# Three of layer 1's modulation groups, computed on VectorE beside layer 0's feed-forward network

## The chip, the core and the metric

The kernel runs on one core of a Trainium2 chip. A core has five engines, each with an instruction queue of its own that it works through in order: TensorE (PE, matrix products; its weight loads are shown apart as PEld), VectorE (DVE), ScalarE (ACT), GpSimd (POOL) and SyncE (SP), which in this kernel issues all DMA transfers. [...] The metric is the device time of one execution in microseconds (us), as the median over several runs.

## The reference

The model is a two-layer backbone over 512 latent tokens with 256 context tokens in front, width 1024. Layer 0 mixes with latent attention (8 heads) and an RWKV-7 recurrence; layer 1 with a state-space scan and windowed attention. Each layer then has a gated feed-forward network. Every norm is modulated by vectors that come from a conditioning vector, one for the latent tokens (c) and one for the context (c_ctx):

```python
def adaln_mods(cond, p):
    return jnp.split(jax.nn.silu(cond) @ p['ada_w'] + p['ada_b'], 6, axis=-1)

def trunk_layer(x_lat, x_ctx, c, c_ctx, p, mixer, rope, need_ctx):
    m_lat = [m[:, None, :] for m in adaln_mods(c, p)]
    m_ctx = adaln_mods(c_ctx, p)
    o_ctx, o_lat = mixer(modulate(x_ctx, p['norm_mix_g'], m_ctx[0], m_ctx[1]),
                         modulate(x_lat, p['norm_mix_g'], m_lat[0], m_lat[1]), p, rope, need_ctx)
    x_lat = x_lat + m_lat[2] * o_lat
    x_lat = x_lat + m_lat[5] * conv_ffn(modulate(x_lat, p['norm_ffn_g'], m_lat[3], m_lat[4]), p)
    if need_ctx:
...
```

So each layer has six groups of 1024 modulation values for each of two conditioning vectors: a product of a 2 x 1024 matrix with a 1024 x 6144 matrix of float32 weights, 4 MB per group. Group 0 is the shift and group 1 the scale of the mixer's norm, group 2 the gate on the mixer's output, groups 3 to 5 the same for the network. In the last layer the context's output isn't needed, so of its groups only 0 and 1 are used.

## The kernel before

Activations lie with features on the 128 partitions and tokens along the free axis (256 context tokens, then 512 latent ones, 768 in all). A float32 product is made of three faster ones: each operand is split into a rounded high part (a copy on ACT) and a remainder (a subtraction on DVE); helper split, lines 386 to 388, does it for activations and load_w, lines 320 to 327, for weights (raw tile wraw, parts whi and wlo; two raw buffers, three split ones).

The modulation of a group is made by ada_group (line 391). For each of 8 blocks of input features it loads a 128 x 1024 weight tile aw (512 KB, line 399) and issues four matmuls into 32-row strips of one PSUM bank; then DVE copies the sums (am, line 404), PE transposes them in two matmuls (line 407) and DVE adds the bias into mods (line 409). The matmuls go through helper mm, so their line is 267.

The program's order is not the written one: a scheduler reorders instructions within each engine by its own estimates, under data dependencies and under explicit ties (issue_after). What the final queue of an engine holds is therefore read from the built program.

The stages that matter here:

- Layer 0's recurrence and attention, about 500 to 735 us of the profiled execution. The recurrence (tiles rec, u, t, b) steps through chunks of 64 tokens in two directions, each step fed by loads of 1 MB (rec) and 128 KB (u). The eight attention heads (tiles kh, qh, ax, ab, pt, o) are interleaved with it on PE. After each of the heads 0, 1 and 2 stands a call of ada_group for layer 1's groups 0, 1 and 2, with a PSUM bank named ad and two aw buffers in a pool aw1.
- The output projection of layer 0, about 735 to 809 us.
- Layer 0's feed-forward network, function ffn, about 810 to 1378 us. Its prenorm has a fill: the call of ada_group for layer 1's group 3 (pool aw2, five buffers). Then it goes through 22 pairs of up tiles in groups of 6, 6, 5 and 5. For each tile PE makes 48 matmuls into one of three accumulators acc; conv3 (lines 380 to 383) drains it with one pass on ACT and two on DVE for each of the two token segments. After each pair come a Silu on ACT, a product on DVE (line 1151) and a split (line 388 on DVE). After each group come eight down tiles, whose results DVE adds to the residual (line 484). The weights are prepared up to three tiles ahead.
- Layer 1's prenorm, from about 1378 us, which needs groups 0 and 1 of mods1, with the call for group 4 (late) beside it.

The few lines that call ada_group:

```python
        if h < 3:
            ada_group(1, h, mods1, "aw1", 2)
...
    ffn(0, mods0, xs, SEG2, NTOK, "left", lambda: ada_group(1, 3, mods1, "aw2", 5))
...
    ada_group(1, 4, mods1, "aw2", 5, late=True)
```

Of the kernel before, what the change touches and what calls it, by code (L numbers as in the profile page):

```python
# [10 lines left out]
F32 = mybir.dt.float32  # L11
F32R = mybir.dt.float32r
AF = mybir.ActivationFunctionType
# [115 lines left out]
def layout(inp):  # L129
# [4 lines left out]
    cc = np.stack([g["c"][0], g["c_ctx"]], 1)  # L134
    a["cc"] = cc.reshape(KT, P, 2).transpose(1, 0, 2)
    a["ada"] = g["ada_w"].reshape(2, KT, P, 6, 1024).transpose(0, 3, 1, 2, 4)
    ab = g["ab_w_in"][0]
    krs = np.concatenate([ab[:, 656:672], ab[:, 640:656]], 1)
    rw = ab[:, 672:]
# [71 lines left out]
def hybrid_kernel(ctx: ExitStack, tc: tile.TileContext, a, out):  # L211
# [44 lines left out]
    ptt = nc.gpsimd.tensor_tensor  # L256

    pace = dict(pins=None, per=0.0, t=0.0, base=0)
    pe_last = [None]

    def mm(o, lhsT, rhs, start, stop, shared=False):
        i = -1
# [122 lines left out]

    def split(hi, lo, src):
        nc.scalar.copy(hi, src)  # L387
        tt(out=lo, in0=src, in1=hi.bitcast(F32), op=ALU.subtract)


    def ada_group(layer, grp, mods, pool, bufs, bank_=None, late=False):
        b = (bank_ or bank)()
        s_ = sc
        if late:
            s_ = F()[:, :KT * 32].rearrange("p (k c) -> p k c", c=32)
            nc.gpsimd.tensor_copy(s_, sc)
        for k in range(KT):
            w = T(pool, [P, 1024], "aw", bufs)
            dma(w, a["ada"][layer, grp, k])
            for g in range(4):  # L400
                mm(b[32 * g:32 * g + 32, :256], lhsT=s_[:, k], rhs=w[:, 256 * g:256 * g + 256], start=k == 0,
                   stop=k == KT - 1)
        am = T(pool, [P, 256], "am", 1)
        nc.vector.tensor_copy(am, b[:, :256])
        b = b[:, 256:]
        for q in range(2):
            nc.tensor.transpose(b[:, q * P:(q + 1) * P], am[:, q * P:(q + 1) * P], ident)
        o = PV[f"ada_b{layer}"] + 8 * grp
        tt(out=mods[:, 8 * grp:8 * grp + 8].rearrange("p (g q) c -> p q g c", q=2),
           in0=b[:, :256].rearrange("p (q g r) -> p q g r", q=2, r=32)[:, :, :, 0:2],  # L410
           in1=pv[:, o:o + 8].rearrange("p (g q) -> p q g", q=2).unsqueeze(3).to_broadcast([P, 2, 4, 2]), op=ALU.add)

    def rstd(ps, n_el, epsi, t0=0, n=NTOK, po=PO, r=None):
        r = F() if r is None else r
# [577 lines left out]
    identr = T("at", [P, P], "identr", 1, F32R)  # L992
    nc.scalar.copy(identr, ident)

    open_pool("aw1", "right")

    def att_load(h):

        t = {}
# [71 lines left out]
    for h in range(8):  # L1071
        cur = nxt
        if h + 1 < 8:
            nxt = att_load(h + 1)
        if h % 2 == 0:
            ot = F()
        att_head(h, ot, *cur)
        if h % 2 and h < 7:
            spill(f"att{h // 2}", ot)
        if h < 3:  # L1080
            ada_group(1, h, mods1, "aw1", 2)
    close_pool("aw1", "at", "mla", "ad", "ob", "ab", "ax")
    open_acc("accm", 2)

    paced(None, 0, 0)
# [28 lines left out]
    close_pool("rwb", "rw1", "rw0", "misc")  # L1114


    def ffn(layer, mods, xs, segs, width, side, fill, nsegs=None, r=None):
        open_pool("ffn", side)

        def S(dt=F32):  # L1120
# [10 lines left out]
        for gsz in FG[layer]:  # L1131
            us, ul = [], []
            halves = layer and j0 + gsz == FT
            for j in range(j0, j0 + gsz):
                cv = []
                for jj in (j, FT + j):
                    ps = acc()
                    dense(ps, next_w("up"), P, hh, hl, segs=segs, by_pass=j < 2)
                    o = S()
                    conv3(o, ps, ALL, col(f"conv_w{layer}0", jj), col(f"conv_w{layer}1", jj), col(f"conv_w{layer}2", jj),  # L1140
                          col(f"conv_b{layer}", jj), segs)
                    cv.append(o)
                    if halves:
                        raw = T("sb", [P, 8, P], "wraw", NWR)
                        dma(raw[:, :gsz], a["down"][layer, len(wb)][:, j0:])
                        hi, lo = [T("hold", [P, 4, P], "w", 16, F32R) for _ in range(2)]
                        split(hi, lo, raw[:, :gsz])
                        wb.append((hi, lo))
                gt, vl = cv
                act(gt[:, n0:], gt[:, n0:], AF.Silu)  # L1150
                tt(out=vl[:, n0:], in0=gt[:, n0:], in1=vl[:, n0:], op=ALU.mult)  # L1151
                hi, lo = S(F32R), S(F32R)
                split(hi[:, n0:], lo[:, n0:], vl[:, n0:])
                us.append(hi)
                ul.append(lo)
            if halves:
                break
            for m in range(8):
                ps = acc()
                dense(ps, next_w("down"), P, us, ul, nk=gsz, segs=segs)  # L1160
                resid(xs[m], ps, mods, 5, m, segs)
            j0 += gsz
# [29 lines left out]
        close_pool("ffn")  # L1192

    open_pool("aw2", "right")
    ffn(0, mods0, xs, SEG2, NTOK, "left", lambda: ada_group(1, 3, mods1, "aw2", 5))


    open_pool("h1", "left")
# [1 line left out]
    for k in range(KT):  # L1200
        dma(xsp[:, k], xs[k][:, L0:L1])
    hh, hl = prenorm(xs, mods1, "norm_mix_g1", 0, 1, lambda: row_tile("h1", "h", 16, F32R), lambda k: xs[k], add=ptt, npool=3)
    ada_group(1, 4, mods1, "aw2", 5, late=True)
    close_pool("aw2", "xs0", "b0", "acc")
    open_pool("sd", "right", psum=True)
    accp[:] = ["acc1", 2, 1024]
# [424 lines left out]
```

## Time and profile before

| | us |
|---|---|
| median of 3 runs | 2265.78 (2265.28 to 2267.42) |
| the profiled execution | 2264.21 |
| its span, first to last instruction | 2262.3 |
| PE busy | 2076.5 |
| DVE busy | 1346.3 |
| ACT busy | 928.3 |
| POOL busy | 506.2 |

The profile is one execution, written down by the hardware. Busy times are of the span; an engine that is busy nearly all the time in a stage sets the pace there, and idle time of another engine costs nothing. Views used below: the page (busy time by engine, the chain of work that ended last), windows (busy time of each engine in stretches of the span, with the granted clock of PE, the busy share of the DMA engines and GB/s), groups of equal instructions with their mean duration, the timeline (start, duration, engine, line, operation, and in brackets the idle time before it and what ended it) and the list of waits (us in total, times, longest).

### The profile page before, as it was taken

How to read it: one execution, taken by the hardware profiler on the slowest of the kernel's cores; microseconds unless marked ns; L12 is line 12 of the kernel's file. 1: busy time of each engine (PE TensorE's matmuls, PEld its weight loads, DVE VectorE, ACT ScalarE, POOL GpSimd, SP SyncE). 2: the span in 40 equal slices, each digit the busy share in tenths (PEclk: the TensorE clock that was granted, in tenths of full speed). 3: DMA queues.
4: the chain of work that ended last, by engine and by line, in shares of the span. 5: the costliest groups of instructions: out<-in, count | busy, mean ns of one | idle time of the engine just before them, and what ended most of it. 6: DMA issues, size and time to landing. Idle time of an engine off the chain costs nothing.

```text
span 2262.3 us, 33884 instructions
## 1 busy us (share of the span) xinstructions
PE 2076.5 (92%) x13558; PEld 1640.9 (73%) x13558; DVE 1346.3 (60%) x2081; ACT 928.3 (41%) x1434; POOL 506.2 (22%) x486
## 2 busy tenths in 40 slices
PE   5888889788998999999999998898888999999997
PEld 3666667566654878888888886786565667888886
DVE  5566965666766465445354444678985556554555
ACT  4445663532355244233132335544344345342434
POOL 0027686611223010000000004442641230000000
PEclk9999999698999999999999999999889999999998
DMA  8477777669741441211212213213426032323231
GB/s 303 125 206 206 182 211 195 211 190 320 259 165 42 154 139 62 61 66 57 75 53 60 75 58 114 96 52 117 133 71 172 28 111 79 96 92 98 84 116 61
DMA packets 181069, 282.58 MB, mean 125 GB/s; under 512 B 63328, under 2 KB 118656, under 8 KB 177840
## 3 DMA queue, kind: packets, MB, share of 16 engines
q1 hardware_dynamic: 180912, 280.42, 40.6%
q8 instruction: 107, 1.75, 0.3%
q14 instruction: 50, 0.41, 0.1%
HBM read 225.43 MB, written 47.33 MB: 121 GB/s over the span
## 4 chain that ended last, share of the span: by engine, by line
PE 65%; DVE 6%; ACT 5%; DMA 5%; issue 3%; POOL 1%; SPq 0%; DVEq 0%; ACTq 0%; POOLq 0%
PE acc L267 49%; PE sd L267 3%; PE o L267 3%; PE wo L267 2%; PE ab L267 2%; PE b L267 2%; DMA u<-sp_v 1%; DVE E L1359 1%; DMA aw<-ada 1%; POOL I L750 1%; PE ax L267 1%; PE ad L267 1%; POOL w L748 1%; DMA E<-sp_ac 1%; ACT L416 1%
## 5 line engine op out<-in xcount | busy, mean ns | idle before, releaser
L267 PE MATMUL acc<-s,whi 128*128 128x512 f32 (+1 forms) x3104 | 759.8, 356 | 3.0 <-ACT s L463 3.0
L267 PEld LDWEIGHTS acc<-s,whi 128*128 128x128 f32 x3104 | 546.0, 188 | 97.3 <-ACT s L463 4.8
L267 PE MATMUL acc<-s,wlo 128*128 128x512 f32 (+1 forms) x1552 | 462.0, 358 | 0.0
L267 PE MATMUL acc<-h,whi 128*128 128x256 f32 (+2 forms) x1248 | 321.1, 371 | 15.9 <-ACT p L639 5.0
L325 ACT CAST whi<-wraw 128x1024 fp32r<-128x1024 f32 (+5 forms) x228 | 210.0, 923 | 282.3 <-PE acc L267 218.0
L267 PEld LDWEIGHTS acc<-s,wlo 128*128 128x128 f32 x1552 | 289.5, 188 | 42.9 <-DVE wlo L326 0.7
L267 PEld LDWEIGHTS acc<-h,whi 128*128 128x128 f32 (+1 forms) x1248 | 223.7, 197 | 68.4 <-issue 15.4
L326 DVE TENSOR_TENSOR wlo<-wraw,whi 128x1024 fp32r<-128x1024 f32 (+5 forms) x205 | 218.7, 1069 | 44.2 <-ACT whi L325 43.6
L381 DVE SCALAR_TENSOR_TENSOR s<-acc,pv,s 128x511 f32<-128x511 f32 (+1 forms) x132 | 87.0, 659 | 246.2 <-ACT s L380 245.4
L380 ACT ACTIVATE s<-acc,pv 128x512 f32<-128x512 f32 (+1 forms) x132 | 93.4, 708 | 235.4 <-PE acc L267 224.2
L484 DVE SCALAR_TENSOR_TENSOR x<-acc,mods,x 128x512 f32<-128x512 f32 (+1 forms) x136 | 79.4, 620 | 175.0 <-PE acc L267 174.8
L267 PE MATMUL acc<-h,wlo 128*128 128x256 f32 (+2 forms) x624 | 179.5, 362 | 0.0
L434 POOL TENSOR_TENSOR f<-f,f 128x768 f32<-128x768 f32 (+1 forms) x24 | 31.3, 1306 | 635.0 <-ACT f L429 625.1
L267 PEld LDWEIGHTS acc<-h,wlo 128*128 128x128 f32 (+1 forms) x624 | 119.3, 195 | 21.9 <-issue 5.6
L1178 POOL TENSOR_TENSOR s<-w,s 128x256 f32<-128x256 f32 x6 | 5.0, 855 | 381.3 <-ACT s L416 381.3
L383 DVE SCALAR_TENSOR_TENSOR s<-acc,pv,s 128x511 f32<-128x511 f32 (+1 forms) x132 | 87.2, 660 | 4.2
L750 POOL TENSOR_TENSOR I<-I,w 128x30 f32<-128x30 f32 (+14 forms) x120 | 76.7, 639 | 9.0
L748 POOL TENSOR_TENSOR w<-I 128x30 f32<-128x30 f32 (+14 forms) x120 | 69.4, 578 | 34.6 <-PE iv L267 25.8
L387 ACT CAST s<-s 128x768 fp32r<-128x768 f32 (+1 forms) x44 | 32.0, 727 | 106.1 <-DVE s L1151 106.1
L326 POOL TENSOR_TENSOR wlo<-wraw,whi 128x1024 fp32r<-128x1024 f32 x23 | 61.7, 2686 | 59.6 <-ACT whi L325 56.1
L1359 DVE TENSOR_SCALAR E<-E,acm 128x128 f32<-128x128 f32 x128 | 61.2, 546 | 14.6 <-ACT G L1356 14.6
L723 DVE TENSOR_TENSOR W<-gk,con 64x512 f32<-64x512 f32 x48 | 32.8, 683 | 51.2 <-ACT PB L722 47.3
(390 smaller groups left out, 3347.3 us busy)
## 6 DMA issues: line engine op xcount, KB each, us to landing
aw<-ada SPq DMA_DIRECT2D x96, 512.0 KB, 5.8
wraw<-up SPq DMA_DIRECT2D x88, 512.0 KB, 3.5
rec<-sp_rec SPq DMA_DIRECT2D x24, 1024.0 KB, 9.7
wraw<-w_in SPq DMA_DIRECT2D x47, 512.0 KB, 3.8
wraw<-down SPq DMA_DIRECT2D x40, 384.0 KB, 3.1
sp_rec<-tg SPq DMA_DIRECT2D x24, 384.0 KB, 3.3
E<-sp_ac SPq DMA_DIRECT2D x16, 512.0 KB, 5.5
x<-xT SPq DMA_DIRECT2D x16, 384.0 KB, 5.9
```

Of the source, the lines that this page charges most:

```text
L267: ins = nc.tensor.matmul(o, lhsT=lhsT, rhs=rhs, start=start, stop=stop, skip_group_check=shared)
L325: nc.scalar.copy(hi[:, :kt], raw[:, :kt])
L326: (eng or tt)(out=lo[:, :kt], in0=raw[:, :kt], in1=hi[:, :kt].bitcast(F32), op=ALU.subtract)
L380: act(o[rows, t0:t0 + n], ps[rows, po:po + n], AF.Identity, scale=w1, bias=b)
L381: stt(out=o[rows, t0 + 1:t0 + n], in0=ps[rows, po:po + n - 1], scalar=w0, in1=o[rows, t0 + 1:t0 + n], op0=ALU.mult, op1=ALU.add)
L383: stt(out=o[rows, t0:t0 + n - 1], in0=ps[rows, po + 1:po + n], scalar=w2, in1=o[rows, t0:t0 + n - 1], op0=ALU.mult, op1=ALU.add)
L387: nc.scalar.copy(hi, src)
L484: stt(out=x[:, t0:t0 + n], in0=ps[:, po:po + n], scalar=mods[:, c6 * 8 + m, c:c + 1], in1=x[:, t0:t0 + n], op0=ALU.mult, op1=ALU.add)
L723: tt(out=w[hk], in0=b[hk].rearrange("p c (a t) -> p c a t", a=2), in1=mk[hk].rearrange("p (a t) -> p a t", a=2).unsqueeze(1).to_broadcast( ...
L748: eng.tensor_tensor(out=tmp, in0=I[:, m + 1:, m:m + 1].to_broadcast([P, n, m]), in1=I[:, m:m + 1, :m].to_broadcast([P, n, m]), op=ALU.mult)
L750: eng.tensor_tensor(out=I[:, m + 1:, :m], in0=I[:, m + 1:, :m], in1=tmp, op=ALU.add)
L1359: ts(out=e[:, h], in0=e[:, h], scalar1=acm[:, c, h0 + h:h0 + h + 1], scalar2=0.0, op0=ALU.subtract, op1=ALU.min)
```

## The change

Groups 0, 1 and 2 of layer 1 are no longer made by ada_group. The weights of these groups are also laid out transposed by the host-side layout (ada1t: 24 tiles of 128 outputs x 1024 inputs), and a new generator ada_rows makes one tile per step: a load of the tile (512 KB) and one scalar_tensor_tensor on DVE that multiplies it with the conditioning vector (srow, loaded to all partitions and put through Silu on ACT) and sums each row into one column of mods1. There are 16 such rows for the context and 24 for the latent tokens, 40 in all, and one addition of the bias after each of the two parts. In ffn of layer 0, from the second pair of up tiles on, two steps of the generator follow each split, and each row is tied behind the split's subtraction on DVE. The pool aw1 goes, and aw2 has four buffers in place of five, plus one for srow.

```diff
@@ layout
+    a["ada1t"] = g["ada_w"][1][:, :3 * D].T.reshape(24, P, D)
+    a["ccrow"] = np.stack([g["c"][0], g["c_ctx"]], 0)
@@ split
-        tt(out=lo, in0=src, in1=hi.bitcast(F32), op=ALU.subtract)
+        dve_last[0] = tt(out=lo, in0=src, in1=hi.bitcast(F32), op=ALU.subtract).ins
@@ new
+    def ada_rows(mods, pool, bufs):
+
+        for c in (1, 0):
+            sr = T(pool, [P, D], "srow", 1)
+            dma(sr, a["ccrow"][c:c + 1].partition_broadcast(P))
+            act(sr, sr, AF.Silu)
+            nt = 16 if c else 24
+            for n in range(nt):
+                w = T(pool, [P, D], "aw", bufs)
+                dma(w, a["ada1t"][n])
+                with tc.issue_after(dve_last[0]):
+                    stt(out=w, in0=w, scalar=1.0, in1=sr, op0=ALU.mult, op1=ALU.mult, accum_out=mods[:, n, c:c + 1])
+                yield
+            tt(out=mods[:, :nt, c], in0=mods[:, :nt, c], in1=pv[:, PV["ada_b1"]:PV["ada_b1"] + nt], op=ALU.add)
@@ attention
-    open_pool("aw1", "right")
...
-        if h < 3:
-            ada_group(1, h, mods1, "aw1", 2)
@@ ffn, behind the split of a pair
+                if beside is not None and j > 0:
+                    next(beside, None)
+                    next(beside, None)
@@ calls
-    ffn(0, mods0, xs, SEG2, NTOK, "left", lambda: ada_group(1, 3, mods1, "aw2", 5))
+    ffn(0, mods0, xs, SEG2, NTOK, "left", lambda: ada_group(1, 3, mods1, "aw2", 4),
+        beside=ada_rows(mods1, "aw2", 4))
...
-    ada_group(1, 4, mods1, "aw2", 5, late=True)
+    ada_group(1, 4, mods1, "aw2", 4, late=True)
```

On PE, in attention head 0 (about 545 us), the queue before holds a step of ada_group (out ad, from aw and the conditioning vector sc) between score matmuls of the head (ab, ax) and a step of the recurrence (b from u and rec):

```order
L267 MATMUL ab_6034<-qh_5915,kh_5909 128x512
L267 MATMUL ab_6034<-qh_5915,kl_5910 128x512
L267 MATMUL ab_6034<-ql_5916,kh_5909 128x512
L267 MATMUL ad_6089<-aw_6102,sc_74 32x256 x4
L267 MATMUL ax_5982<-kh_5958,qh_5964 128x256 x2
L267 MATMUL b_4767<-u_4621,rec_4620 64x64 x3
L267 MATMUL b_4356<-rec_4161,u_4162 64x64 x16
L267 MATMUL b_4767<-u_4621,rec_4620 64x64 x5
```

The same place after the change (numbers in names differ from build to build, and lines stand two further down):

```order
L269 MATMUL ab_6031<-qh_5912,kh_5906 128x512
L269 MATMUL ab_6031<-qh_5912,kl_5907 128x512
L269 MATMUL ab_6031<-ql_5913,kh_5906 128x512
L269 MATMUL b_4767<-u_4621,rec_4620 64x64 x7
L269 MATMUL b_4356<-rec_4161,u_4162 64x64 x16
L269 MATMUL b_4767<-u_4621,rec_4620 64x64
L269 MATMUL ax_5979<-kh_5955,qh_5961 128x256 x2
```

The ad step is gone, and the scheduler has also exchanged the recurrence step with the next head's ax; such exchanges run through the whole stage, on DVE, ACT and SP as well.

On DVE, in the network, before: the product and the split of a pair (s), then the next tile's convolution (s from acc) with the remainder of a weight tile (wlo) in its middle:

```order
L1151 TENSOR_TENSOR s_8139<-s_8077,s_8139 128x768
L388 TENSOR_TENSOR s_8149<-s_8139,s_8148 128x768
L381 SCALAR_TENSOR_TENSOR s_8207<-acc_8152,pv_71,s_8207 128x255
L383 SCALAR_TENSOR_TENSOR s_8207<-acc_8152,pv_71,s_8207 128x255
L326 TENSOR_TENSOR wlo_8218<-wraw_8215,whi_8217 128x1024
L381 SCALAR_TENSOR_TENSOR s_8207<-acc_8152,pv_71,s_8207 128x511
L383 SCALAR_TENSOR_TENSOR s_8207<-acc_8152,pv_71,s_8207 128x511
```

After, at a pair's end:

```order
L390 TENSOR_TENSOR s_8122<-s_8112,s_8121 128x768
L426 SCALAR_TENSOR_TENSOR aw_8125,mods_7_76<-aw_8125,srow_7986 128x1024
L426 SCALAR_TENSOR_TENSOR aw_8128,mods_7_76<-aw_8128,srow_7986 128x1024
L383 SCALAR_TENSOR_TENSOR s_8186<-acc_8131,pv_71,s_8186 128x255
L328 TENSOR_TENSOR wlo_8197<-wraw_8194,whi_8196 128x1024
L385 SCALAR_TENSOR_TENSOR s_8186<-acc_8131,pv_71,s_8186 128x255
L383 SCALAR_TENSOR_TENSOR s_8186<-acc_8131,pv_71,s_8186 128x511
L385 SCALAR_TENSOR_TENSOR s_8186<-acc_8131,pv_71,s_8186 128x511
```

Two row sums stand between the split and the next convolution, and wlo now comes one place earlier in that convolution. Each row's tile is loaded by SP, whose queue holds in the network, after the change:

```order
L324 DMA wraw_8132<-up 128x1024
L424 DMA aw_8261<-ada1t 128x1024
L424 DMA aw_8264<-ada1t 128x1024
L324 DMA wraw_8194<-up 128x1024
L324 DMA wraw_8268<-up 128x1024
L424 DMA aw_8397<-ada1t 128x1024
L424 DMA aw_8400<-ada1t 128x1024
```

Before, only the loads of wraw stood there. The two loads of aw wait for free buffers, that is for the rows of two pairs earlier.

More of the change, by code (lines that the diff above doesn't have):

```diff
@@ L258, in hybrid_kernel @@
     pace = dict(pins=None, per=0.0, t=0.0, base=0)
-    pe_last = [None]
+    pe_last, dve_last = [None], [None]
     def mm(o, lhsT, rhs, start, stop, shared=False):
@@ L1079, in hybrid_kernel @@
             spill(f"att{h // 2}", ot)
-        if h < 3:
-            ada_group(1, h, mods1, "aw1", 2)
-    close_pool("aw1", "at", "mla", "ad", "ob", "ab", "ax")
+    close_pool("at", "mla", "ad", "ob", "ab", "ax")
     open_acc("accm", 2)
@@ L1114, in hybrid_kernel, with ffn @@
     close_pool("rwb", "rw1", "rw0", "misc")
-    def ffn(layer, mods, xs, segs, width, side, fill, nsegs=None, r=None):
+    def ffn(layer, mods, xs, segs, width, side, fill, nsegs=None, r=None, beside=None):
         open_pool("ffn", side)
```

## The prediction

> **What bounds the kernel now.** I read the page first, then tables by stage, because the change takes work from one stage and puts it into another.
>
> ```profile
> PE 2076.5 (92%) x13558; PEld 1640.9 (73%) x13558; DVE 1346.3 (60%) x2081; ACT 928.3 (41%) x1434; POOL 506.2 (22%) x486
> PE 65%; DVE 6%; ACT 5%; DMA 5%; issue 3%; POOL 1%; SPq 0%; DVEq 0%; ACTq 0%; POOLq 0%
> ```
>
> TensorE (PE) is the main limit and VectorE (DVE) has room on average. An average proves nothing for a stage, so here is the stage that loses work (recurrence and attention, 500 to 750 us): core time, then busy time of PE, PE's weight loads, DVE, ACT and POOL, clock and DMA.
>
> ```profile
> 500.00:540.00 40.00, 31.86 (x574) 25.56 (x573) 27.80 (x62) 11.56 (x26) 0.00 (x0) 0.87 1.04 328
> 540.00:580.00 40.00, 36.89 (x460) 24.31 (x458) 24.92 (x47) 11.43 (x23) 12.36 (x9) 0.91 1.02 308
> 580.00:620.00 40.00, 39.32 (x557) 26.34 (x555) 28.87 (x60) 12.23 (x25) 10.52 (x9) 1.00 0.70 232
> 620.00:660.00 40.00, 39.23 (x416) 23.73 (x414) 26.83 (x50) 16.72 (x28) 12.05 (x10) 1.00 0.58 195
> 660.00:700.00 40.00, 32.49 (x293) 19.74 (x288) 30.82 (x51) 20.01 (x30) 12.14 (x9) 0.96 0.18 60
> 700.00:750.00 50.00, 43.99 (x237) 27.77 (x236) 30.96 (x46) 28.94 (x41) 13.83 (x11) 0.97 0.44 150
> ```
>
> From 580 to 660 PE is busy 78.55 of 80 us: there it alone sets the pace. From 500 to 580 the DMA engines are full (share above 1) and PE idles 11 us. From 660 to 750 PE is busy 76.5 of 90 us, so chains through ACT and DVE set part of the pace.
>
> The stage that receives the work is layer 0's feed-forward network. In the chain that ended last it is one piece, and the sum over fourteen windows from 828 to 1380 us says the same:
>
> ```profile
> 828.47 549.63 PE acc L267 x3129
> ```
>
> ```profile
> sum 552.00, PE 551.64 PEld 482.38 DVE 264.32 ACT 169.63 POOL 16.85; mean PE 39.40 PEld 34.46 DVE 18.88 ACT 12.12 POOL 1.20
> ```
>
> PE never waits there, and DVE works 48% of the time. Work on DVE costs nothing here until it delays something that PE needs.
>
> **What leaves the attention stage.** Three calls of ada_group: on PE 24 weight tiles (each a step of four small matmuls, which the trace counts as 8 records) and three pairs of transposes; on SP 24 loads of 512 KB; on DVE three copies and three sums of under half a microsecond. PE's part by 40 us, from the windows on tile ad (PE, its weight loads, DVE):
>
> ```profile
> 500.00:540.00 40.00, 1.99 (x16) 0.58 (x16) 0.00 (x0) 0.87 1.04 328
> 540.00:580.00 40.00, 4.27 (x48) 0.99 (x48) 0.00 (x0) 0.91 1.02 308
> 580.00:620.00 40.00, 6.57 (x66) 1.81 (x66) 1.01 (x3) 1.00 0.70 232
> 620.00:660.00 40.00, 6.95 (x68) 2.10 (x68) 0.59 (x2) 1.00 0.58 195
> ```
>
> These 19.8 us hold tails that overlap the next matmul. What a step takes from the path is the distance to the next start, in PE's timeline:
>
> ```profile
> 564.55 1.08 PE L267 MATMUL ad<-aw,sc 128*32 128x256 f32 x8 [3.06 <-DMA aw<-ada]
> ...
> 575.62 0.64 PE L267 MATMUL ad<-aw,sc 128*32 128x256 f32 x8
> 576.19 0.65 PE L267 MATMUL o<-pt,vt 128*64 128x256 f32 x4
> ...
> 621.12 0.44 PE L407 MATMUL ad<-con,am 128*128 128x128 f32 x2
> 621.31 0.48 PE L267 MATMUL ab<-ql,kh 128*128 128x512 f32 x1
> ```
>
> 576.19 - 575.62 = 0.57 us a step, so 24 x 0.57 = 13.7 us; a pair of transposes 0.19 us, three 0.6. **PE term: 14.3 us.**
>
> Next, waits. The chain charges two long pieces to these loads:
>
> ```profile
> 535.27 11.01 DMA aw<-ada
> 553.23 11.28 DMA aw<-ada
> ```
>
> They look like 22 us to win, but run from issue to landing, and PE did other work meanwhile. What PE really waited for is in its list of waits, 500 to 580 us and then 660 to 750 us:
>
> ```profile
> PE b L267 <- DVE u L827: 4.7, 2, 3.0
> PE ad L267 <- DMA aw<-ada: 3.1, 1, 3.1
> PE b L267 <- DVE t L836: 3.0, 3, 1.4
> ```
>
> ```profile
> PE b L267 <- DVE u L827: 4.5, 1, 4.5
> ```
>
> **Wait term: 3.1 us** for the loads themselves. Eight of the 24 loads (4.2 MB, about 13 us at 315 GB/s) are issued between 511 and 566 us into full DMA engines, beside the u and rec loads of the recurrence, on which DVE's u depends. How much of the 4.7 us goes is not shown: between 0 and 4.7; I take 1.5, nearer zero, since the first long u loads were issued before any aw load. Gross: 14.3 + 3.1 + 1.5 = 18.9 us.
>
> Not all of that reaches the end of the stage: what is late next are the attention heads' own chains after 660 us, where PE is busy 76.5 / 90 = 85%. I carry 85% over: **16.1 us**. Bounds: 25% of the PE term plus the wait, 6.7 us; everything plus both u waits, 14.3 + 3.1 + 4.7 + 4.5 = 26.6 us.
>
> **What the feed-forward network gets.** 40 row sums on DVE, two per pair of up tiles, 40 loads of 512 KB, two broadcast loads with a Silu on ACT, two small additions. No such row sum stands in the trace. The nearest rows are scalar_tensor_tensor from two float32 SBUF tensors, and the dearest one of that kind:
>
> ```profile
> L462 DVE SCALAR_TENSOR_TENSOR x<-x,gs,f 128x512 f32<-128x512 f32 x16 | 11.9, 742 | 0.0
> L462 DVE SCALAR_TENSOR_TENSOR x<-x,gs,f 128x256 f32<-128x256 f32 x16 | 7.6, 476 | 8.0 <-ACT f L416 8.0
> ```
>
> ```profile
> L682 DVE SCALAR_TENSOR_TENSOR p<-p,p x8: 1002/2160/2615, 119.3 to 337.5; 128x768 f32<-128x768 f32 x8
> ```
>
> 256 elements more cost 266 ns, so 1024 cost 742 + 2 x 266 = 1274 ns; at the dearest rate 2615 x 1024 / 768 = 3.49 us. I take 1.27 (POOL, busy beside line 682, rests here): 51 us on DVE, 2.5 us per pair. The cover is in DVE's timeline (in brackets the idle time before a row):
>
> ```profile
> 864.70 0.48 DVE L381 SCALAR_TENSOR_TENSOR s<-acc,pv,s 128x255 f32<-128x255 f32 x1 [1.63 <-ACT s L380]
> ...
> 873.12 0.48 DVE L381 SCALAR_TENSOR_TENSOR s<-acc,pv,s 128x255 f32<-128x255 f32 x1 [4.82 <-ACT s L380]
> ...
> 878.68 0.96 DVE L388 TENSOR_TENSOR s<-s,s 128x768 fp32r<-128x768 f32 x1 [0.96 <-ACT s L387]
> 881.55 0.48 DVE L381 SCALAR_TENSOR_TENSOR s<-acc,pv,s 128x255 f32<-128x255 f32 x1 [1.92 <-ACT s L380]
> ```
>
> A pair lasts 881.55 - 864.70 = 16.85 us, of which DVE idles 4.82 + 0.96 + 1.92 = 7.7. The rows start right behind the split of line 388, at 879.64, and run to about 882.2: the next convolution starts 0.6 us late, and the following gap of 4.82 takes that up. Queued behind a row are that convolution (it frees one of three accumulators) and the next wlo (weights are prepared three tiles ahead, a tile is 8.42 us). **Cost: 0**; even at 3.49 us two rows are 7.0 of 7.7. Without this cover the 51 us would stand on the path.
>
> SP issues everything in order. A row's load waits until DVE has read the tile four rows back, and weight loads stand behind it. With two buffers wraw such a load is issued two tiles, some 16 us, before its cast, so a hold of a few microseconds is hidden; a longer one would be paid in full. The first Silu stands among ACT's casts for the output projection, with a table load:
>
> ```profile
> 753.98 0.62 ACT L325 CAST whi<-wraw 128x512 fp32r<-128x512 f32 x1 [4.65 <-PE acc L267]
> ...
> 815.75 1.28 ACT L416 ACT_TABLE_LOAD   x1
> ```
>
> ACT idles 4.65 us ahead of such a cast, so 1.28 us and about 1 us for the Silu fit: 0, else 2.3 us once.
>
> [...]
>
> **Small losses.** The buffers aw of groups 3 and 4 go from five to four, so one more load of each comes late:
>
> ```profile
> 815.87 9.05 SPq L399 DMA_DIRECT2D aw<-ada  x8
> ...
> 823.89 0.64 PE L267 MATMUL b<-aw,sc 128*32 128x256 f32 x8
> ```
>
> ```profile
> 1383.79 1.29 SPq L399 DMA_DIRECT2D aw<-ada  x3
> ...
> 1393.84 0.64 PE L267 MATMUL b<-aw,f 128*32 128x256 f32 x8
> ```
>
> The last steps stand between matmuls that wait for ACT's s and h anyway. One more issue is 0.4 us (1.29 / 3); I charge 0.5 at each place, 1 in all, bounds 0 and 4.
>
> **Sum.** 2264.2 (the profiled execution) - 16.1 + 1.0 = 2249.1; that execution lies 1.6 us under the median of 2265.8, so 2250.7 by the median, given as 2250.5.
>
> **Rivals.**
> 1. *The removed matmuls were filler.* They stand between steps of the recurrence, and PE would now wait there instead. For it: 11 us of idle PE from 500 to 580, and the waits on u and t. Against it: 13.5 of the 19.8 us lie in 580 to 660, where PE is never free. Gain then 6.7 - 1 = 5.7: 2260. The clock belongs here: it is 0.87 to 0.91 where PE waits and 1.00 where it is full; 80 us at 0.91 would return 7 us. [...]
> 2. *More goes than I count.* All bounds at once, and no 4.5 us stall at 697: 26.6 - 1, giving 2240.
> 3. *DVE becomes the bound of the network* (slower). It decides when two rows exceed 7.7 us, 3.85 us a row; each 0.1 us above costs 40 x 0.1 = 4 us. At 4.6 us a row it is 30 us, less 15.1: 2281. Against it: the dearest comparable row is 3.49 us.
>
> That the change doesn't do what it says is excluded by the order: the ad steps are gone and the 40 rows stand behind the splits.
>
> **Chances.** Forecast (2246 to 2256) 0.62; larger gain 0.13; filler 0.18, half of it within 0.2%, which is 4.5 us and about what a measurement can tell from no change; slower 0.07. Faster: 0.62 + 0.13 + 0.09 = 0.84; same 0.09; slower 0.07. The range leaves out the slower case and little else: 2238 to 2263.
>
> **What would show it.** Right: PE still busy in all windows of the network; row sums near 1.3 us; the stretch from 500 us to the start of the network about 16 us shorter. Wrong: PE waits on wlo or acc between 830 and 1370 us; windows near 600 us with PE well under 39 of 40; new waits of the recurrence on u loads.

## The result, and the profile after

The changed kernel takes 2254.94 us (median of 5 runs, 2251.5 to 2259.24); the kernel before took 2267.13 us beside it (median of 5). The ratio is 0.9945, with a 95% interval of 0.9933 to 0.9957: 12 us gained, where 15 were forecast, and inside the forecast range.

The profiled execution is the slowest of the five, 2259.24 us (span 2257.2). Its first page lines, busy time by engine and the chain that ended last:

```profile
PE 2066.3 (92%) x13360; PEld 1636.3 (72%) x13360; DVE 1393.8 (62%) x2157; ACT 930.8 (41%) x1437; POOL 506.2 (22%) x486
PE 64%; DVE 7%; ACT 5%; DMA 4%; issue 3%; POOL 1%; SPq 1%; DVEq 0%; ACTq 0%; POOLq 0%
```

PE has lost 10.2 us of busy time, DVE has gained 47.5. To see where the time went, one needs points that both programs pass. Here are the last inverse in front of the recurrence (iv), the last product of the attention (ad from pt) and the first matmul of modulation group 3, which stands just ahead of the network (b from aw). First and last start are given in us, of the kernel before:

```profile
L267 PE MATMUL iv<-PN,PB x384: 218/228/258, 244.0 to 480.6; 32*32 32x32 f32 x192
L267 PE MATMUL ad<-pt,ones x8: 272/273/273, 734.8 to 735.1; 128*64 128x128 f32 x8
L267 PE MATMUL b<-aw,sc x64: 379/379/636, 814.7 to 824.2; 128*32 128x256 f32 x64
```

and of the changed kernel:

```profile
L269 PE MATMUL iv<-PN,PB x384: 218/228/258, 248.3 to 485.7; 32*32 32x32 f32 x192
L269 PE MATMUL ad<-pt,ones x8: 417/418/418, 731.0 to 731.6; 128*64 128x128 f32 x8
L269 PE MATMUL b<-aw,sc x64: 379/392/636, 805.8 to 817.5; 128*32 128x256 f32 x64
```

The part ahead of the inverse, which the change does not touch, came 5.1 us later in this run. From there to group 3 it was 814.7 - 480.6 = 334.1 us and is 805.8 - 485.7 = 320.1: **14.0 us shorter**. Of these, 8.6 go before the attention's last product (254.5 to 245.9) and 5.4 behind it (79.6 to 74.2), at the head of the output projection. I call this stretch "inverse to group 3" below. The rest of the program differs by 3.8 us the other way in these two runs, while the medians differ by 12.2.

The windows of the changed kernel over the stage that lost work (the columns are those of the prediction):

```profile
500.00:540.00 40.00, 31.94 (x491) 26.97 (x489) 27.57 (x57) 11.42 (x25) 0.00 (x0) 0.79 1.03 321
540.00:580.00 40.00, 37.37 (x530) 26.87 (x531) 29.13 (x60) 13.30 (x27) 11.36 (x9) 1.00 0.85 258
580.00:620.00 40.00, 37.28 (x566) 27.31 (x564) 31.58 (x63) 14.03 (x30) 10.67 (x9) 1.00 0.40 129
620.00:660.00 40.00, 36.92 (x347) 23.10 (x345) 30.15 (x52) 18.16 (x31) 13.98 (x11) 1.00 0.41 139
660.00:700.00 40.00, 34.44 (x265) 22.05 (x263) 30.22 (x46) 23.55 (x34) 10.15 (x9) 0.91 0.15 51
700.00:750.00 50.00, 44.38 (x241) 29.58 (x240) 32.40 (x44) 22.89 (x34) 13.77 (x10) 0.97 0.38 134
sum 250.00, PE 222.34 PEld 155.88 DVE 181.04 ACT 103.36 POOL 59.93; mean PE 37.06 PEld 25.98 DVE 30.17 ACT 17.23 POOL 9.99
```

Two columns tell a story that the prediction did not have. From 580 to 660 us PE was busy 78.55 of 80 us; it is now 74.2 (37.28 and 36.92 of 40), so PE did not simply close up: it waits a little there. That is one of the signs of being wrong that the prediction had named. And the DMA engines, full until 580 us before (1.02, then 0.70), are now at 0.85 from 540 and 0.40 from 580. The recurrence's matmuls (b from rs and rec; 336 of the 384 stand behind the last inverse, and only these are counted), before and after, show what else moved:

```profile
L267 PE MATMUL b<-rs,rec x336: 218/218/367, 486.3 to 690.8; 64*64 64x64 f32 x168
```

```profile
L269 PE MATMUL b<-rs,rec x336: 217/218/367, 491.4 to 671.4; 64*64 64x64 f32 x168
```

This part of the recurrence, called its length below, takes 180.0 us in place of 204.5. So two theories stood against each other: **PE's time** (the 96 matmuls and the transposes, as the prediction had it) and **the loads** (24 times 512 KB on DMA engines and a queue that the recurrence needs).

The stage that received the work: the network's piece of the chain, windows on it, and the new rows by group (busy time, mean ns of one, idle time ahead):

```profile
821.41 548.41 PE acc L269 x3123
```

```profile
sum 540.00, PE 539.81 PEld 472.81 DVE 301.63 ACT 168.88 POOL 16.15; mean PE 179.94 PEld 157.60 DVE 100.54 ACT 56.29 POOL 5.38
```

```profile
L426 DVE SCALAR_TENSOR_TENSOR aw<-aw,srow 128x1024 f32<-128x1024 f32 x40 | 47.3, 1218 | 0.0
L426 DVE DVE_READ_ACCUMULATOR aw<-aw,srow 128x1 f32 x40 | 3.3, 81 | 0.0
```

PE is busy 539.81 of 540 us (830 to 1370); the piece is 548.41 us against 549.63. No instruction of PE waited in that window.

### The profile page after: what moved, and what is told of

Its sections match the earlier page's. It is cut to its first block, busy times and chain, and to the rows that moved or that the text cites. A ratio compares the mean times of both kernels' runs of the same rounds, so it can differ in the third digit from the quotient of the medians.

```text
span 2257.2 us, 33584 instructions
## 1 busy us (share of the span) xinstructions
PE 2066.3 (92%) x13360; PEld 1636.3 (72%) x13360; DVE 1393.8 (62%) x2157; ACT 930.8 (41%) x1437; POOL 506.2 (22%) x486
## 4 chain that ended last, share of the span: by engine, by line
PE 64%; DVE 7%; ACT 5%; DMA 4%; issue 3%; POOL 1%; SPq 1%; DVEq 0%; ACTq 0%; POOLq 0%
PE acc L269 50%; PE sd L269 3%; PE b L269 3%; PE o L269 2%; PE ab L269 2%; PE wo L269 2%; DVE E L1376 2%; DMA E<-sp_ac 1%; PE ax L269 1%; POOL I L767 1%; DMA rec<-sp_rec 1%; POOL w L765 1%; ACT L433 0%; PE iv L269 0%; PE gk L269 0%
## 5 line engine op out<-in xcount | busy, mean ns | idle before, releaser
L269 PE MATMUL acc<-s,wlo 128*128 128x512 f32 (+1 forms) x1552 | 456.4, 354 | 0.0
```

What stands on the lines that cost most here:

```text
L269: ins = nc.tensor.matmul(o, lhsT=lhsT, rhs=rhs, start=start, stop=stop, skip_group_check=shared)
```

## The experiments

Each was timed in 5 rounds beside the kernel before; ratios are to that kernel, and the changed kernel's own 0.9945 is the mark. The diffs are against the changed kernel, unless said.

**1. Nothing on DVE.** The row sums are left out, and with them layer 1's first three groups, which stay zero.

```diff
+    nc.vector.memset(mods1, 0.0)
...
-        beside=ada_rows(mods1, "aw2", 4))
```

> The kernel after the change without the 40 row sums and their loads (groups 0 to 2 of layer 1 are left at zero); attention has the same order on PE. Theory (the rows are wholly hidden in the feed-forward network, the gain is all from attention): the same time as after the change, ratio to before 0.9945 within 0.001. Rival (the rows cost something, which is why the gain is 12 us and not the 16 to 18 us that left attention): 4 to 6 us less, ratio about 0.992.

Measured: 2255.83 us, ratio 0.994 (0.9927 to 0.9953). The 40 rows, their loads and the Silu cost nothing that can be told from zero. The two intervals alone would still hide some 5 us (0.9945 against 0.994, each with some 0.0012 to either side); that no instruction of PE waited in the network, as shown above, speaks against even that.

**2. Groups back in the attention, rows kept too.** The groups' results go to scratch.

```diff
+    open_pool("aw1", "right")
...
+        if h < 3:
+            ada_group(1, h, mdum, "aw1", 2)
```

> The kernel after the change with the three groups also computed in attention as before (into a scratch tile), so PE's order there is almost that of before, and with the 40 rows in the network. Theory (rows free): the time of before, ratio 1.000 within 0.0015. Rival (rows cost 4 to 6 us): ratio about 1.002 to 1.0025.

Measured: 2267.38 us, ratio 0.9994 (0.9983 to 1.0004). With the groups back the whole gain is gone. So, as far as the interval tells, all of it comes out of the attention stage, and the rows take nothing from it.

**3. The matmuls without the loads.** As 2, but all steps read one tile that is loaded once.

```diff
-            w = T(pool, [P, 1024], "aw", bufs)
-            dma(w, a["ada"][layer, grp, k])
+            if still is None:
...
+            else:
+                w = still
...
+    dma(wst, a["ada"][1, 0, 0])
...
+            ada_group(1, h, mdum, "aw1", 2, still=wst)
```

> After the change, with the matmuls, transposes and DVE steps of the three groups put back into attention, but on one resident weight tile (24 loads become 1; the results are not used). Theory A (PE's 14.3 us are most of the gain): 10 to 14 us slower than after, ratio to before 0.9990 to 1.0000. Theory B (the loads, which fill the DMA engines, are most of it): 2 to 5 us slower than after, ratio 0.996.

Measured: 2259.92 us, ratio 0.9957 (0.9943 to 0.9971). PE does the same steps and transposes as before, and some 3 us (0.0012 x 2268) are lost, an amount within the two intervals. The steps no longer wait for loads, so they also stand elsewhere: from 531.8 to 597.2 us, in the kernel before from 525.3 to 654.9. Run 7 comes back to that.

**4. The loads without the matmuls, read by POOL.**

```diff
+        if h < 3:
+            for k in range(KT):
+                w = T("aw1", [P, 1024], "aw", 2)
+                dma(w, a["ada"][1, h, k])
+                nc.gpsimd.tensor_copy(mdum[:, 0:1, 0], w[:, 0:1])
```

> After the change, with the 24 loads of 512 KB put back into attention into two buffers, each read by a copy of one column on POOL, and no matmuls. Theory A: 0 to 4 us slower than after, ratio to before 0.9945 to 0.9965. Theory B: 8 to 12 us slower, ratio 0.998 to 1.000.

Measured: 2275.86 us, ratio 1.0033 (1.002 to 1.0045): worse than the kernel before. It says little about the loads. From 500 to 750 us POOL's copies waited 72.3 us for these loads, with the attention's sums sm behind them in its queue, and PE waited 12.7 us for the sums. The reader of a load has to be one that would wait for it anyway, so the next try reads it on PE.

**5. The loads with a quarter of the matmuls.** One 32x256 matmul a load in place of four, no transposes.

```diff
+        if h < 3:
+            b = bank()
+            for k in range(KT):
+                w = T("aw1", [P, 1024], "aw", 2)
+                dma(w, a["ada"][1, h, k])
+                mm(b[:32, :256], lhsT=sc[:, k], rhs=w[:, :256], start=k == 0, stop=k == KT - 1)
+            nc.vector.tensor_copy(mdum[:32, :, 0], b[:32, :48])
```

> The changed kernel with the 24 loads of 512 KB back in the attention heads, two buffers, each read by a single 32x256 matmul (24 of 96, no transposes; their results go to scratch). Theory that the loads cost, by bytes or by their place in SP's queue: ratio to before 0.998 to 1.000, nearly as the kernel with the groups back whole (0.9994). Theory of PE's time, as the prediction had it: 72 matmuls and the transposes gone, three quarters of 14.3 us, so ratio about 0.995 to 0.996.

Measured: 2268.32 us, ratio 0.9996 (0.9987 to 1.0005). Three quarters of the matmuls and all transposes are gone, and nothing is won; 3 and 5 together settle it against PE's time as the main part of the gain. From 540 to 620 us the DMA engines are again as full as in the kernel before, and the recurrence is nearly as long again, 197.3 us:

```profile
540.00:580.00 40.00, 37.44 (x479) 26.37 (x480) 22.23 (x50) 13.06 (x26) 10.93 (x9) 0.91 1.04 314
580.00:620.00 40.00, 37.44 (x473) 24.81 (x471) 28.65 (x58) 10.47 (x22) 8.39 (x8) 1.00 0.77 243
```

```profile
L269 PE MATMUL b<-rs,rec x336: 217/218/268, 490.5 to 687.8; 64*64 64x64 f32 x168
```

The next question was what of a load costs: its bytes, or its wait for a buffer in SP's queue, behind which the recurrence's loads stand.

**6 and 7. The waits without the bytes.** As 3, with 24 loads of 16 KB in two buffers. In the first form they came from a copy of the vector operand, stored at the program's start; in the second from 32 columns of the weights, and one more 32x32 matmul reads each of 21 of them. The diff is that of the second.

```diff
+            else:
+                w = still
+                l = T(pool, [P, 32], "lw", bufs)
+                dma(l, a["ada"][layer, grp, k][:, :32])
...
+                if still is not None and g == 0 and k > 0:
+                    mm(b[:32, :32], lhsT=s_[:, k], rhs=l, start=False, stop=False)
```

> The changed kernel with the three groups' matmuls and transposes back in the attention heads, as the kernel before has them, on one resident weight tile; but with 24 loads of 16 KB (the vector operand, in two buffers) in the places of the 24 loads of 512 KB. So the wait of SP's queue for PE to give up a buffer is kept, and the bytes are not. Theory of bytes (the 12.6 MB on the DMA engines hold up the recurrence's loads): as the kernel with the matmuls on a resident tile and no loads, ratio to before about 0.9957. Theory of the queue (SP's waits for a buffer stand in front of the recurrence's loads, whatever their size): as the kernel with the groups back whole, ratio about 0.9994. A third outcome, in between, would split the cost.

> As the run with 24 small loads, without its change at the program's start: the changed kernel with the three groups' matmuls and transposes back in the attention heads on one resident weight tile, and 24 loads of 16 KB (32 columns of the weights, two buffers) in the places of the 24 of 512 KB; 21 of them are read by one more 32x32 matmul each, so that the queue still waits for PE to give up a buffer. From the first attention score to the third of the groups behind (the matmul that starts group 3) the kernel with matmuls and no loads took 278 us, the one with the groups back whole 285, the changed kernel 275. Theory of bytes: 278 and ratio to before about 0.9957. Theory of the queue's waits for PE: 285 and ratio about 0.9994.

Measured: the first 2262.24 us, ratio 0.997 (0.996 to 0.998); the second 2257.54 us, ratio 0.9952 (0.994 to 0.9965). The first lies between the theories. Its store changes the start of the program too: in its profiled run the last inverse starts at 466.7 us, 13 us and more ahead of all others, and the stretch from there to group 3 is 12 us longer than in the changed kernel. That profiled execution took 2251.89 us, 10 us under the median, so it stands badly for the run, and what the store changes was not followed up; the second form has no such change. In SP's list of waits from 440 to 740 us (total, times, longest), line 829 is the recurrence's own record load, which waits for PE in the changed kernel too (78.7 us); line 406 is the small load, line 399 the large one in the kernel before:

```profile
SPq L829 <- PE b L269: 43.9, 9, 10.8
...
SPq L406 <- PE ad L269: 29.4, 11, 6.4
```

```profile
SPq L399 <- PE ad L267: 15.1, 12, 3.8
```

So the queue waits for PE at the small loads about as often as at the large ones, and longer. But the DMA engines are as free as in the changed kernel (0.84 and 0.39 from 540 and 580 us), and nothing measurable is lost, though the recurrence is 187.6 us long and not 180. In this run the queue's waits were free. It also answers for PE's time a second time, by its window from 580 us and the sum from 500 to 750 us:

```profile
580.00:620.00 40.00, 40.00 (x578) 27.33 (x578) 29.02 (x64) 11.87 (x25) 9.45 (x8) 1.00 0.39 120
sum 250.00, PE 229.28 PEld 158.20 DVE 178.53 ACT 101.23 POOL 60.91; mean PE 38.21 PEld 26.37 DVE 29.75 ACT 16.87 POOL 10.15
```

PE is busy 7 us more than in the changed kernel's 222.34, and full from 580 to 620 us, and the stretch from inverse to group 3 is no longer (319.1 us against 320.1): the steps fit into PE's idle time.

**8 and 9. The bytes without the waits.** 24 copies of 512 KB from memory to memory, two in front of each of the recurrence's last twelve record loads. They need no buffer on the core. In the first form all record loads were tied one behind the other, in the second, whose diff this is, only the last twelve.

```diff
-        dma(r, REC[q][:, i])
+        pin = sp_last[0]
+        if i >= 6:
+            for k in range(2):
+                with tc.issue_after(pin):
+                    pin = dma(cp_d[q, i - 6, k], a["ada"][1, q, i - 6]).ins
+        with tc.issue_after(pin) if i >= 6 else nullcontext():
+            sp_last[0] = dma(r, REC[q][:, i]).ins
```

> The changed kernel with the bytes and without the waits: 24 copies of 512 KB of the same weights from memory to memory, two in front of each of the recurrence's last twelve record loads on SP's queue, where the kernel before has its 24 loads. They need no buffer on the core, so the queue waits for nobody at them; no matmul reads them. Theory of bytes (the recurrence's loads land late because the DMA engines are busy): ratio to before about 0.999 to 1.000, and the recurrence, from its first to its last step on the records, takes 200 us or more in place of the changed kernel's 180. Theory of the queue's waits for PE: as the changed kernel, ratio about 0.9945, the recurrence 180 us.

> The changed kernel with 24 copies of 512 KB from memory to memory, two in front of each of the recurrence's last twelve record loads on SP's queue, as in the run before; but the first twelve record loads keep their places in SP's queue (in the run before they were tied one behind the other, and the recurrence began 50 us late). Bytes without waits for a buffer and without matmuls. Theory of bytes: ratio to before 0.998 to 1.001, the recurrence 195 us or more from its first to its last step (180 in the changed kernel). If it is again well over 1.001, copies from memory to memory take more from the DMA engines than loads do, and the run bounds the cost only from one side. If bytes alone cost nothing: 0.9945 and 180 us.

Measured: the first 2281.74 us, ratio 1.0054 (1.0041 to 1.0068), the second 2263.7 us, ratio 0.9973 (0.9963 to 0.9984). In the first the ties held back the early record loads: the recurrence's first matmuls start at 414.0 us, as they do elsewhere, but the next only at 507.2 (428.3 in the second form), so it tells nothing of the bytes. The second fits neither theory. The DMA engines are as busy as the expectation wanted:

```profile
540.00:580.00 40.00, 35.99 (x483) 25.94 (x483) 28.12 (x50) 13.86 (x27) 14.16 (x11) 0.96 0.93 350
580.00:620.00 40.00, 37.59 (x528) 27.72 (x528) 28.89 (x59) 14.22 (x29) 11.96 (x10) 0.96 0.86 317
```

and half of the gain is lost (0.0028 of 0.0055, 6 us), but the recurrence is hardly longer:

```profile
L269 PE MATMUL b<-rs,rec x336: 218/218/366, 488.2 to 672.0; 64*64 64x64 f32 x168
```

183.8 us, where 195 or more were expected. So the copies cost, and not by way of the recurrence's length. That it is their bytes is likely but not shown: a copy is also written to memory and takes longer than a load (9.5 us from issue to landing against 6.5, last section), the DMA engines are busy at other times (0.89 from 500 to 540 us and 0.86 from 580, where the kernel before has 1.04 and 0.70), and the last twelve record loads are tied to the copies.

**10. The kernel before, with its 24 loads late.** Nothing goes to DVE; the loads are tied behind the last record load. The diff is against the kernel before.

```diff
-            dma(w, a["ada"][layer, grp, k])
+            with tc.issue_after(sp_last[0]) if pool == "aw1" else nullcontext():
+                dma(w, a["ada"][layer, grp, k])
...
-        dma(r, REC[q][:, i])
+        sp_last[0] = dma(r, REC[q][:, i]).ins
```

> The kernel before, with nothing moved to DVE: only its 24 loads of the three groups are tied behind the recurrence's last record load on SP's queue, so that they go out from about 630 us on, where the DMA engines are 0.4 busy and less, and not among the record loads from 511 us on. The same loads, waits, matmuls and transposes. Theory of bytes in the way of the recurrence: the recurrence ends at 670 to 680 us on the records, as without the loads, and PE's 3 us for the matmuls stay: ratio 0.995 to 0.997. Theory that the three groups cost by PE's time, or by the loads wherever they stand: ratio about 1.000. A loss (over 1.001) would come from the groups' last matmuls or the output projection's weights, which then stand behind the loads at the end of the attention.

Measured: 2262.77 us, ratio 0.9966 (0.9954 to 0.9979). Another order of the loads, with all the work still on PE, brings 0.0034 of the 0.0055 (by its interval 0.0021 to 0.0046). The matmuls move with their loads, though: they stand at 635.5 to 719.7 us in place of 525.3 to 654.9, and the run doesn't part the one from the other. The recurrence is as short as in the changed kernel, and the DMA engines are as free early (0.83 and 0.39 from 540 and 580 us). At the late loads (line 402) SP waits for PE and for the loads themselves; its 27.0 us for wlo stand in the kernel before as well:

```profile
L267 PE MATMUL b<-rs,rec x336: 218/218/366, 490.5 to 669.3; 64*64 64x64 f32 x168
```

```profile
SPq L402 <- PE ad L267: 46.0, 15, 5.5
SPq L322 <- DVE wlo L326: 27.0, 6, 10.8
SPq L402 <- DMA aw<-ada: 19.2, 10, 4.2
```

The heads' own loads and the output projection's weights now stand behind them. That this is where the other 5 us go (0.0021 x 2268) was not tried, and the profiled execution, 2267.78 us and 5 us above the median, can't show where the gain lies.

**11. Four times the rows.** Each row sum is done four times, the repeats into a scratch column: eight row operations a pair.

```diff
+                    for _ in range(3):
+                        stt(out=w, in0=w, scalar=1.0, in1=sr, op0=ALU.mult, op1=ALU.mult, accum_out=dum)
```

> The changed kernel with every row sum done four times (the repeats into a scratch column): eight row operations a pair in place of two, 9.2 us by the 1.15 us from start to start that the trace shows, against 7.7 us spare in a pair of 16.85 us. If DVE's spare time is the bound: about 1.5 us more a pair at 20 pairs, 30 us longer than the changed kernel, 2285, ratio to before 1.008; and PE shows new waits on DVE's splits. If the tied rows cost something long before DVE is full, or if the spare time is larger than its gaps, it comes out elsewhere: up to 20 pairs times 9.2 = 184 us if nothing of them is hidden, 0 if all is.

Measured: 2264.29 us, ratio 0.9983 (0.9975 to 0.9992), 9 us more than the changed kernel and not 30. PE's list of waits from 830 to 1370 us has a single line, and windows of 20 us show where the waits stand, at the end of the first group of six pairs:

```profile
PE acc L269 <- DVE s L385: 8.3, 4, 2.8
```

```profile
870.00:890.00 20.00, 20.00 (x116) 17.55 (x115) 18.78 (x31) 6.27 (x8) 0.00 (x0) 1.00 0.37 119
890.00:910.00 20.00, 20.00 (x116) 17.54 (x115) 19.39 (x32) 6.90 (x10) 0.00 (x0) 1.00 0.28 93
910.00:930.00 20.00, 18.16 (x95) 15.56 (x94) 19.97 (x36) 5.14 (x7) 0.00 (x0) 0.91 0.22 73
930.00:950.00 20.00, 20.00 (x116) 17.54 (x115) 11.49 (x19) 2.50 (x3) 0.00 (x0) 1.00 0.50 165
```

DVE (third time in a row) fills up over the pairs of the group, 18.8, 19.4, 20.0 of 20 us, and PE waits only at its end. Then come the down tiles, where DVE has little to do, and it starts afresh. There are four such groups of pairs, and four waits of 1.2 to 2.8 us. The bound on DVE lies between four rows a pair (free in the next run) and eight; the change uses two.

**12. All six groups as rows.** Four rows a pair, 64 in all, and no modulation matmul of layer 1 left on PE.

```diff
-    ffn(0, mods0, xs, SEG2, NTOK, "left", lambda: ada_group(1, 3, mods1, "aw2", 4),
+    ffn(0, mods0, xs, SEG2, NTOK, "left", None,
...
-    ada_group(1, 4, mods1, "aw2", 4, late=True)
...
-    ffn(1, mods1, xs, SEGX, NLAT, "left", lambda: ada_group(1, 5, mods1, "aw3", 8, acc), SEGH, r1)
+    ffn(1, mods1, xs, SEGX, NLAT, "left", None, SEGH, r1)
...
-            nt = 16 if c else 24
+            nt = 16 if c else 48
...
-                    next(beside, None)
-                    next(beside, None)
+                    for _ in range(4):
+                        next(beside, None)
```

> A version that may beat both: all six groups of layer 1's modulation as row sums behind the splits of layer 0's network, four a pair (64 rows), and nothing of them left on PE as filler (the group in layer 0's network, the late one, and the one in layer 1's network go). If PE's time for a group is about 1 us where it lies in other work, as the experiment with resident weights gives (3 us for three), and the last group's chain at the end of layer 0's network goes too: 2 to 6 us shorter than the changed kernel, ratio to before 0.992 to 0.9935. If four rows a pair (4.6 of 7.7 us spare) already disturb the splits, or the 32 MB of rows hold up the network's weights: same or longer than the changed kernel, ratio 0.9945 or over.

Measured: 2259.11 us, ratio 0.9952 (0.9939 to 0.9964): no better than the changed kernel. In the chain that ended last the network is now in two pieces:

```profile
803.26 21.80 PE acc L269 x111
...
831.36 531.13 PE acc L269 x3024
```

The second is 17 us shorter than the changed kernel's one piece, but only because the chain breaks once at 831 us. From the network's first matmul on the chain to the end of that piece it is 559.2 us (803.26 to 1362.49), against 559.7 in the changed kernel (810.12 to 1369.82): the network is no shorter. It begins 4.0 us sooner behind the last inverse, and what follows it takes 4.5 us longer. Four rows a pair disturb nothing (PE waits 0.4 us on DVE in the network). So nothing is won in all by taking the last groups off PE; that they had filled places at which PE waits for a norm anyway is a likely reason, and was not tried apart.

## Why the prediction came out right, and which step of it did not

**Cost 0 in the network: shown.** The row took 1.218 us where 1.27 was worked out, and PE stayed full. The timeline of DVE shows two rows behind a pair's split (line 390) and in front of the next convolution, as the order had them:

```profile
853.56 0.96 DVE L390 TENSOR_TENSOR s<-s,s 128x768 fp32r<-128x768 f32 x1 [0.96 <-ACT s L389]
854.43 1.22 DVE L426 SCALAR_TENSOR_TENSOR aw<-aw,srow 128x1024 f32<-128x1024 f32 x1
855.58 0.08 DVE L426 DVE_READ_ACCUMULATOR aw<-aw,srow 128x1 f32 x1
855.58 1.22 DVE L426 SCALAR_TENSOR_TENSOR aw<-aw,srow 128x1024 f32<-128x1024 f32 x1
856.72 0.08 DVE L426 DVE_READ_ACCUMULATOR aw<-aw,srow 128x1 f32 x1
856.72 0.48 DVE L383 SCALAR_TENSOR_TENSOR s<-acc,pv,s 128x255 f32<-128x255 f32 x1
```

Run 1 (no rows) gives the same time, run 12 shows that double the number is free too, run 11 that four times is not. The first Silu, the row loads and SP's queue in the network cost nothing either, by run 1. The 1274 ns were an estimate from rows without an accumulator; with one, and two float32 sources, the 40 rows took 1215 to 1222 ns for 1024 elements.

**PE term, 14.3 us, of which 85% were carried: the step that failed.** "There it alone sets the pace" was read from 78.55 busy us of 80. The steps on a resident tile cost 3 us by run 3 and 2 by run 7 (0.0007 x 2268), both within the intervals, and removing three quarters of the matmuls with the loads kept (run 5) brings nothing. That PE is full does not show that it sets the end of the stage, and the reading rule that stands with the profile before fails here: in run 7 PE is busy 40.00 of 40 us from 580 to 620, and the stretch is no longer than in the changed kernel, where it is busy 37.28. The likely reason is that PE had work then that could also be done at another time. The distance of 0.57 us between two steps was read correctly, but is not what a step costs.

**Wait term, 3.1 us.** PE's wait for aw is gone, as forecast. What it was worth by itself was not measured apart from the loads. That 85% of all this reaches the end of the stage was a guess that no run tests.

**u and DMA term, 1.5 us: mis-sized, and looked for in the wrong line.** PE's wait on u did not change: in the list from 505 to 585 us it is

```profile
PE b L269 <- DVE u L844: 4.6, 2, 2.9
```

against 4.7 us before. The 4.5 us stall on u at 697 us, which only the upper bound had counted, is gone; it is there in run 2 (4.5 us) and down to 0.6 us in run 5, so it does not go with the loads alone. The loads' cost is not in that line. Run 2 lies 0.0037 above run 3 (the same matmuls, without the loads), 8 us; run 5 lies 0.0051 above the changed kernel (loads and a quarter of the matmuls), 11.6 us, of which the matmuls would be about 1. So the loads with their waits, counted as 4.6 us in the gross sum, are worth 8 to 11, and PE's steps, counted as 14.3, about 3. The two errors nearly cancel. That the total came out, 14.0 us from inverse to group 3 in the two profiles where 16.1 were forecast, and 12 by the medians where 15 were, is luck.

**Small losses, 1.0 us.** From group 3 to the late group 4 the profiled runs take 568.4 and 569.0 us: 0.6, within the bounds of 0 to 4, and too small to be told from the runs' scatter.

**Rivals.** That the matmuls were filler (the first) was right in its mechanism; its price of 5.7 us was wrong, because it took the loads' worth from the list of waits. The clock that it feared for is 0.79 and 1.00 in the first two windows (0.87 and 0.91 before), lower in the one and higher in the other, the first at nearly the same busy time of PE (31.94 us, 31.86 before). From 580 to 660 us, where PE now idles 5.8 of 80 us, it stays 1.00. The 7 us rest on the clock following PE's idle time, which was the author's estimate and which no run shows. Of the second, one part came true: the stall at 697 us is gone. That DVE would become the bound fell with the row's duration.

**What stays open** is how the loads cost their 8 to 11 us. Small loads with the same kind of waits are free (run 7); copies of as many bytes without waits cost 6 us and leave the recurrence short (run 9), and its profile has the loss behind the attention's last product, 83.5 us to group 3 in place of 74.2; large loads with waits cost the most and lengthen the recurrence to 197 us and more (runs 2 and 5); moved behind the record loads they cost 5 us and leave it short (run 10). So bytes and waits together cost more than each alone, and the length of the recurrence goes with the time in some runs and not in others (187.6 us in run 7, which lost nothing, 183.8 in run 9, which lost 6). In each of these kernels the scheduler also puts PE's instructions in another order, and what that is worth was not separated. No run fixed the order and changed the loads alone.

## What to carry to other kernels

A stretch in which an engine is busy nearly all the time isn't shown to be bound by it: where a scheduler moves work about, put the engine's work back without its loads before you count each removed step as time. The lists of waits show the last releaser; here they gave 3.1 us to loads that were worth 8 to 11, so look at the DMA column of the stage and at who shares the queue as well. And before work is moved to another engine, try moving its loads, and with them the work that reads them, out of the crowded stretch: here that brought some 60% of the gain.

## What the runs showed of the hardware

The accumulator's result is read by an instruction of its own, DVE_READ_ACCUMULATOR, 81 ns; the next row starts 1.15 us behind the one before it (854.43 to 855.58), so the pair costs less than the two durations added (1218 + 81 ns). Copies of 512 KB from memory to memory, all 24 issued between 500 and 660 us, took 9.5 us from issue to landing in run 9, against 6.5 for loads of 512 KB to the core, issued between 511 and 650 us in the kernel before, by the medians of their groups of DMA issues:

```profile
sp_cp<-ada SPq DMA_DIRECT2D x24, 512.0 KB, 9.5
```

```profile
aw<-ada SPq DMA_DIRECT2D x24, 512.0 KB, 6.5
```
